# Fetching the experts' token rows with an indirect DMA instead of 0/1 products

## The chip, the cores and the metric

The kernel runs on one core of a Trainium2 chip. The metric is the device time of one execution in microseconds. The kernel before took 1614.17 us (median of 3 runs).

## The reference

A decoder trunk of two layers over 256 tokens of width 1024, in float32. The second layer's channel mixer is a top-2-of-8 expert SwiGLU:

```
logits = h @ w_router                                 # h = rms_norm(x)
top_val, top_idx = lax.top_k(logits, 2); top_w = softmax(top_val)
combine = sum(one_hot(top_idx, 8) * top_w[..., None], axis=-2)
for e in range(8):
    y += combine[..., e:e+1] * swiglu(h, w_gate_e[e], w_up_e[e], w_down_e[e])
x = x + y
```

The inner width of an expert is 3584. A final RMSNorm follows.

## The kernel before, in words

Every weight is float32 and is streamed once from device memory in units of 128 x 2048 elements (1 MiB), through a ring of slots (class `Stream`; its loads are issued on SyncE's queue, line 142). A unit is used in two halves. `do_split` cuts a half into a rounded part `wh` (ScalarE, line 152) and the rest `wl` (VectorE, line 153). `take` keeps four halves of splits ahead of the half that TensorE is about to use; five pairs of buffers hold them. `run` issues the products of a half: for each block of 512 columns one of the activations' high part and one of their low part with `wh` (lines 256 and 257), and after all blocks one with `wl` for each (line 261).

All instructions are issued in one order that the program itself plans. It counts an estimated clock: `run` calls `tick` after each block, with 512/1200 us for a pair of products with `wh` and 512/2400 for one with `wl`. Side work is put into a queue with `soon(wait, fn)` or `later(wait, fn)`, and the next `tick` at or past its time issues it between the weight products. Each engine then runs its own instructions in that order.

The experts come after both attention layers. `route` works out which tokens go to which expert, with a slot number for each. An expert has 7 chunks (j = 0 to 6) of 512 inner columns. In a chunk TensorE does two units for the gate, two for the up projection and two of the chunk before for the down projection (`down`). Four transposes turn the product g (`g_transpose`, line 884); lines 330 and 331 copy them out. Up to 128 tokens of an expert are worked on in one pass, as columns of `th` and `tl`, the high and the low part of the normed activations; the columns of even and of odd experts lie side by side.

What the next expert needs is prepared by `expert_prep` (lines 764 to 809), which is put into the side queue at the end of chunk j = 2. `select` makes the 0/1 matrix G (VectorE, line 772): token t is in slot s. `gather(q)`, called twice, multiplies the residual `xs` with G (line 780; two token blocks of 128 for each of 4 column blocks), which gives the rows of the expert's tokens, already turned; ScalarE and VectorE copy them into `th` and `tl` with the norm's gain (lines 784 and 787). `trans` turns G for the later scatter (line 802). `scales` multiplies G with `rc`, which holds each token's 1/rms and its weight for the expert (line 796), and VectorE copies the result (line 797). The planner's waits are

```
p1=4.0, p2=6.0, p3=8.0, p4=9.0      # gather(0), gather(1), trans, scales; select has 0.0
```

For the first expert the same steps run right behind `route`, ahead of all expert products.

GpSimd does small powers alone (line 327, 1/rms, and line 756, in the weights of the routing). Line 336 adds a mixer's output to `xs`; line 844 adds an expert's output to the result, which lies in a buffer of its own, so that `xs` stays as it is while the experts run.

Of the kernel before, what the change touches and what calls it, by code (L numbers as in the profile page):

```python
# [11 lines left out]
F32 = mybir.dt.float32  # L12
F32R = mybir.dt.float32r
BF16 = mybir.dt.bfloat16
I32 = mybir.dt.int32
# [4 lines left out]
P = 128  # L20
S = 256
D = 1024
# [87 lines left out]
C_LT = C_SIN + 128  # L110
C_IOTA = C_LT + 64
C_WR = C_IOTA + 128
C_ALL = C_WR + 64
B_TRI = 4 * 384
B_ONE = B_TRI + 128
B_ALL = B_ONE + 128
# [54 lines left out]
def trunk(ctx: ExitStack, tc: tile.TileContext, x, xt, wpre, wmoe, cst, cstb, gfin, out):  # L171
    nc = tc.nc
# [58 lines left out]
    def soon(wait, fn):  # L231
        put(urgent, wait, fn)
# [82 lines left out]
    def norm_half(gi, c):  # L315
# [6 lines left out]
        if gi != 3 or c == 0:  # L322
            soon(at + 1, lambda: sumsq(xs, c))

    def make_rstd():
        V.scalar_tensor_tensor(ms, ss[:, :, 0], EPS, ss[:, :, 1], op0=ALU.add, op1=ALU.add)  # L326
        nc.gpsimd.tensor_tensor(rstd, ms, nhalf, op=ALU.pow)  # L327
# [11 lines left out]
    def mixer(i, gnext, last=False):  # L339
        oo = [[], []]  # L340

        def out_unit(kh, c):
            unit((th, tl), oo[c], 4 * kh, 4, 512, kh == 0, kh == 1)

        with tc.tile_pool(name=f"mix{i}", bufs=2) as mp:
            with tc.tile_pool(name=f"att{i}", bufs=2, side="right", reuse_waits="tile") as ap:
                gates = attention(mp, ap)
            if last:
                moe_ring()
            projections(mp, gates)  # L350
            oo[0] += [mm_ps(), mm_ps()]
            out_unit(0, 0)
            oo[1] += [mm_ps(), mm_ps()]
            out_unit(0, 1)
            flush()
        if last:
            moe_open()
        for c in range(2):
            out_unit(1, c)
            flush()  # L360
            add_x(oo[c], c)
            norm_half(gnext, c)
            if c == 0 and last:
                soon(5.0, lambda: logits(0))

    def attention(mp, ap):
# [334 lines left out]
    def route():  # L701
        ep = M["ep"]

        def small(shape, name, dt=F32):
            return ep.tile(shape, dt, name=name, bufs=1)

        lp = M["lp"]
        lo, L, v8 = small([P, 2, 8], "lo"), small([P, 2, 8], "L"), small([P, 2, 8], "v8")
        R = ep.tile([P, 2, P], F32, name="G", tag="G")
        R1, R2 = (R[:, i, :].rearrange("p (b e j) -> p b e j", b=2, e=8) for i in range(2))  # L710
        rank = small([P, 2, 8], "rank")
        sel, slot = small([P, 2, 8], "sel", BF16), small([P, 2, 8], "slot")
        d1, z = small([P, 2, 8], "d1"), small([P, 2, 8], "z")
        rc = small([P, 2, 8, 2], "rc")
        warm(10)
        for b in range(2):
            A.activation(lo[:, b, :], lp[b][:, 8:16], AF.Copy, scale=rstd[:, b:b + 1])
        for b in range(2):
            V.scalar_tensor_tensor(L[:, b, :], lp[b][:, 0:8], rstd[:, b:b + 1], lo[:, b, :],
                                   op0=ALU.mult, op1=ALU.add)  # L720

        lt = C[:, C_LT:C_LT + 64].rearrange("p (e j) -> p e j", e=8).unsqueeze(1).to_broadcast([P, 2, 8, 8])
        lj = L.unsqueeze(2).to_broadcast([P, 2, 8, 8])
        le = L.unsqueeze(3).to_broadcast([P, 2, 8, 8])
        V.tensor_tensor(R2, lj, le, op=ALU.is_equal)
        V.tensor_tensor(R1, lj, le, op=ALU.is_gt)
        V.tensor_tensor(R2, R2, lt, op=ALU.mult)
        V.tensor_tensor(R1, R1, R2, op=ALU.add)
        V.tensor_reduce(rank, R1, axis=AX.X, op=ALU.add)
        V.tensor_scalar(sel, rank, 1.5, None, op0=ALU.is_lt)  # L730
        for b in range(2):
            V.tensor_copy(rc[:, b, :, 0], rstd[:, b:b + 1].to_broadcast([P, 8]))

        pp = mm_ps()
        tri, one = CB[:, 0:128], CB[:, 128:256]
        T.matmul(pp[:, 0:8], tri, sel[:, 0, :], start=True, stop=True)
        T.matmul(pp[:, 8:16], one, sel[:, 0, :], start=True, stop=False)
        T.matmul(pp[:, 8:16], tri, sel[:, 1, :], start=False, stop=True)
        T.matmul(pp[:, 16:24], one, sel[:, 0, :], start=True, stop=False)
        T.matmul(pp[:, 16:24], one, sel[:, 1, :], start=False, stop=True)  # L740
        V.tensor_tensor(slot, pp[:, 0:16].rearrange("p (b e) -> p b e", b=2), sel, op=ALU.mult)
        M["slot"], M["rc"] = slot, rc

        def weights():
            most, mosti = small([P, 1], "most"), small([P, 1], "mosti", I32)
            V.tensor_reduce(most, pp[:, 16:24], axis=AX.X, op=ALU.max)
            V.tensor_copy(mosti, most)
            M["most"] = mosti
            for b in range(2):
                V.max(v8[:, b, :], L[:, b, :])  # L750

            for b in range(2):
                V.tensor_scalar(d1[:, b, :], L[:, b, :], -2.0, v8[:, b, 0:1], op0=ALU.mult, op1=ALU.add)
            for b in range(2):
                V.tensor_scalar(z[:, b, :], d1[:, b, :], v8[:, b, 1:2], 88.0, op0=ALU.add, op1=ALU.min)
            nc.gpsimd.tensor_tensor(z, base_e.unsqueeze(2).to_broadcast([P, 2, 8]), z, op=ALU.pow)

        def weights2():
            V.tensor_scalar(z, z, 1.0, None, op0=ALU.add)
            V.reciprocal(z, z)  # L760
            V.tensor_tensor(rc[:, :, :, 1], z, sel, op=ALU.mult)
        return weights, weights2

    def expert_prep(e, off):

        ep, par = M["ep"], e % 2
        sl = {}

        def select():
            sl["G"] = ep.tile([P, 2, P], F32, name="G", tag="G")  # L770
            for b in range(2):
                V.tensor_scalar(sl["G"][:, b, :], C[:, C_IOTA:C_IOTA + P], float(off), M["slot"][:, b, e:e + 1],
                                op0=ALU.add, op1=ALU.is_equal)

        def gather(q):
            p = tp_ps()
            for i in range(4):
                k = 4 * q + i
                for b in range(2):
                    T.matmul(p[:, i * P:(i + 1) * P], xs[:, b, k * P:(k + 1) * P], sl["G"][:, b, :],  # L780
                             start=b == 0, stop=b == 1)
            for i in range(4):
                k = 4 * q + i
                A.activation(th[:, k, par * P:(par + 1) * P], p[:, i * P:(i + 1) * P], AF.Copy, scale=gain(3, k))
            for i in range(4):
                k = 4 * q + i
                V.scalar_tensor_tensor(tl[:, k, par * P:(par + 1) * P], p[:, i * P:(i + 1) * P], gain(3, k),
                                       th[:, k, par * P:(par + 1) * P].bitcast(F32),
                                       op0=ALU.mult, op1=ALU.subtract)

        def scales(c0, c1):
            if not c0:
                sl["sc"] = ep.tile([P, 2], F32, name="sc", tag="sc")
            p = tp_ps()
            for b in range(2):
                T.matmul(p[:, c0:c1], sl["G"][:, b, :], M["rc"][:, b, e, c0:c1], start=b == 0, stop=b == 1)
            V.tensor_copy(sl["sc"][:, c0:c1], p[:, c0:c1])

        def trans():
            p = tp_ps()  # L800
            for b in range(2):
                T.transpose(p[:, b * P:(b + 1) * P], sl["G"][:, b, :], ident)
            sl["GT"] = ep.tile([P, S], F32R, name="GT", tag="GT")
            A.activation(sl["GT"], p[:, 0:S], AF.Copy)

        M["slots", e] = sl
        both = (0, 1, 2) if e == 0 and not off else (0, 2)
        return [select, lambda: gather(0), lambda: gather(1), trans,
                *(lambda c=c: scales(*c) for c in zip(both, both[1:]))]

# [37 lines left out]
    def experts(off, first, weights=()):  # L848
# [11 lines left out]
        for e in range(NE):  # L860
            for j in range(NCH):
# [26 lines left out]
                    down(*prev, first and prev[0] == 0)  # L888
                prev = (e, j, gT)
                if j == 2 and e + 1 < NE:  # L890
                    for wait, fn in zip((0.0, PAR['p1'], PAR['p2'], PAR['p3'], PAR['p4']), expert_prep(e + 1, off)):
                        later(wait, fn)
                if j == NCH - 1:
                    drain()
# [2 lines left out]

    wrhl = base.tile([P, 8, 16], F32R, name="wrhl")
    M = {"ring": []}
    zeros = base.tile([P, P], BF16, name="zeros")  # L900
    V.memset(zeros, 0.0)

# [32 lines left out]
    flush()  # L935
    warm(4)
    make_rstd()
    logits(1)
    experts(0, True, route())

# [28 lines left out]
def constants(inputs):  # L969
# [14 lines left out]
    for i, n in enumerate(("norm_mix_0", "norm_ffn_0", "norm_mix_1", "norm_ffn_1")):  # L984
        c[:, C_G + 8 * i:C_G + 8 * i + 8] = inputs[n].reshape(8, P).T
    c[:, C_WR:C_WR + 64] = inputs["w_router_1"].reshape(8, P, NE).transpose(1, 0, 2).reshape(P, 64)
    b = np.zeros((P, B_ALL), np.float32)
    t = np.arange(S)[:, None]
    s = np.arange(S)[None, :]
    d = t - s  # L990
# [39 lines left out]
```

## Time and profile before

| | |
|---|---|
| runs | 1612.93, 1614.17, 1614.98 us |
| profiled execution | 1613.7 us |
| its span, first to last instruction | 1611.9 us |
| granted TensorE clock | 0.996 of full speed |
| busy TensorE / VectorE / ScalarE / GpSimd | 99% / 80% / 68% / 0% of the span |
| moved | 456.17 MB |

Times in rows are microseconds from the first instruction, and durations are in microseconds unless a column says ns. TensorE's products are pipelined, so a row's duration is longer than the distance to the next; that distance is what a product costs. PE is TensorE's products, PEld its loads of the stationary operand, DVE is VectorE, ACT is ScalarE, POOL is GpSimd and SP is SyncE, whose queue issues the transfers.

### The profile page before, as it was taken

Reading aid. Unit: us, or ns where it says so; the run is one execution under the profiler, and the core shown is the slowest. Engines: PE = TensorE matmul, PEld = TensorE weight load, DVE = VectorE, ACT = ScalarE, POOL = GpSimd, SP = SyncE. Lnnn points to the kernel's source line nnn. Section 1 sums busy time; section 2 is a strip of 40 time slices with the busy share of each in tenths; the row PEclk is TensorE's granted clock in tenths of the full one; section 3 lists DMA queues with packets and bytes.
Section 4 is the critical chain, followed back from the end, with each engine's and each line's share of the span. In section 5 each row is a group of like instructions: output and inputs, shape, how many; then the busy total and the mean of one; then the engine's idle time right before and its main releaser. Section 6 shows DMA issues by size and latency. Waiting matters only on the chain. (4 is left out here: it accounts for less than half of the span.)

```text
span 1611.9 us, 21105 instructions
## 1 busy us (share of the span) xinstructions
PE 1593.9 (99%) x7661; PEld 1306.4 (81%) x7661; DVE 1293.2 (80%) x1654; ACT 1096.8 (68%) x1413; POOL 6.6 (0%) x10
## 2 busy tenths in 40 slices
PE   9999999999999999999999999999999999999996
PEld 7777888888877878888888888888888888888885
DVE  6767655555786668899899889889889899889996
ACT  6556454445556448777787787787777777787784
POOL 0000000000000000000000000000000000000000
PEclk9999999999999999999999999999999999999998
DMA  8443546555434596899899899899999899989960
GB/s 333 171 144 141 182 174 198 185 185 200 167 144 148 217 395 246 332 365 361 336 378 355 339 368 353 335 361 360 340 375 352 341 368 363 362 335 364 361 261 28
DMA packets 64305, 456.17 MB, mean 283 GB/s; under 512 B 7104, under 2 KB 7360, under 8 KB 9408
## 3 DMA queue, kind: packets, MB, share of 16 engines
q1 hardware_dynamic: 64192, 454.73, 74.6%
q8 instruction: 62, 1.02, 0.2%
q14 instruction: 51, 0.42, 0.1%
HBM read 453.66 MB, written 1.05 MB: 282 GB/s over the span
## 5 line engine op out<-in xcount | busy, mean ns | idle before, releaser
L256 PE MATMUL mm<-wh,th 128*128 128x512 f32 (+1 forms) x1536 | 604.3, 395 | 2.0 <-ACT wh L152 2.0
L257 PE MATMUL mm<-wh,tl 128*128 128x512 f32 (+1 forms) x1536 | 592.3, 387 | 0.0
L153 DVE TENSOR_TENSOR wl<-raw,wh 128x1024 fp32r<-128x1024 f32 x376 | 447.2, 1221 | 135.3 <-ACT wh L152 134.8
L152 ACT ACTIVATE wh<-raw 128x1024 fp32r<-128x1024 f32 x376 | 390.9, 1058 | 148.3 <-PE mm L257 113.9
L261 PE MATMUL mm<-wl,th 128*128 128x512 f32 (+1 forms) x1536 | 451.5, 390 | 0.0
L153 DVE TENSOR_TENSOR wl<-ringa,wh 128x1024 fp32r<-128x1024 f32 x290 | 340.5, 1220 | 27.9 <-ACT wh L152 27.8
L256 PEld LDWEIGHTS mm<-wh,th 128*128 128x128 f32 x1536 | 289.2, 188 | 62.9 <-issue 5.7
L257 PEld LDWEIGHTS mm<-wh,tl 128*128 128x128 f32 x1536 | 289.6, 189 | 54.3
L261 PEld LDWEIGHTS mm<-wl,th 128*128 128x128 f32 x1536 | 281.5, 189 | 57.7 <-issue 2.0
L152 ACT ACTIVATE wh<-ringa 128x1024 fp32r<-128x1024 f32 x290 | 299.6, 1062 | 33.9 <-PE mm L257 16.1
L153 DVE TENSOR_TENSOR wl<-ringb,wh 128x1024 fp32r<-128x1024 f32 x188 | 217.7, 1220 | 19.4 <-ACT wh L152 19.4
L152 ACT ACTIVATE wh<-ringb 128x1024 fp32r<-128x1024 f32 x188 | 193.0, 1062 | 22.9 <-PE acc L257 13.5
L256 PE MATMUL acc<-wh,gT 128*128 128x512 f32 x224 | 87.4, 390 | 0.0
L257 PE MATMUL acc<-wh,gT 128*128 128x512 f32 x224 | 87.3, 390 | 0.0
L257 PE MATMUL acc<-wh,tmp 128*128 128x512 f32 x224 | 87.3, 390 | 0.0
L256 PE MATMUL acc<-wh,tmp 128*128 128x512 f32 x224 | 87.3, 390 | 0.0
L261 PE MATMUL acc<-wl,gT 128*128 128x512 f32 x224 | 69.2, 390 | 0.0
L261 PE MATMUL acc<-wl,tmp 128*128 128x512 f32 x224 | 69.2, 390 | 0.0
L867 ACT ACTIVATE g<-mm,sc 128x512 f32<-128x512 f32 x56 | 38.7, 691 | 39.4 <-PE mm L261 39.4
L261 PEld LDWEIGHTS acc<-wl,gT 128*128 128x128 f32 x224 | 42.1, 188 | 8.8
L257 PEld LDWEIGHTS acc<-wh,gT 128*128 128x128 f32 x224 | 42.1, 188 | 8.8
L257 PEld LDWEIGHTS acc<-wh,tmp 128*128 128x128 f32 x224 | 42.1, 188 | 8.7
(178 smaller groups left out, 1257.7 us busy)
## 6 DMA issues: line engine op xcount, KB each, us to landing
ringa<-in_wmoe_dram SPq DMA_DIRECT2D x144, 1024.0 KB, 6.1
raw<-in_wmoe_dram SPq DMA_DIRECT2D x96, 1024.0 KB, 5.8
ringb<-in_wmoe_dram SPq DMA_DIRECT2D x94, 1024.0 KB, 6.2
raw<-in_wpre_dram SPq DMA_DIRECT2D x91, 1024.0 KB, 4.8
late<-in_wmoe_dram SPq DMA_DIRECT2D x2, 1024.0 KB, 7.8
raw<-in_wpre_dram SPq DMA_DIRECT2D x2, 512.0 KB, 6.0
xs<-in_x_dram SPq DMA_DIRECT2D x2, 512.0 KB, 7.9
ringa<-in_wpre_dram SPq DMA_DIRECT2D x1, 1024.0 KB, 6.8
```

The source lines that it names most:

```text
L152: self.nc.scalar.activation(h, s, AF.Copy)
L153: self.nc.vector.tensor_tensor(l, s, h.bitcast(F32), op=ALU.subtract)
L256: T.matmul(o, xh(b), wh, start=start, stop=False)
L257: T.matmul(o, xl(b), wh, start=False, stop=False)
L261: T.matmul(o, xh(b), wl, start=False, stop=stop)
L867: A.activation(g, og, AF.Silu, scale=sl["sc"][:, 0:1])
```

## The change

The residual stream `xs` is also written to a buffer `xd` in device memory, in two halves, from GpSimd's queue. For experts 2 to 8, `scales` moves to the place right behind `select` and has a third column: the token's number. VectorE turns it into 32-bit integers, and GpSimd issues an indirect DMA that fetches the row of `xd` that each slot names into the tile `xg` (a slot without a token names row 0). `gather` then is four transposes of `xg` for each half in place of eight products with G. The waits of the preparation are new. The first expert is prepared as before.

```diff
+    def store_x(c):
+        nc.gpsimd.dma_start(M["xd"].rearrange("(b p) d -> p b d", p=P)[:, :, c * 512:(c + 1) * 512],
+                            xs[:, :, c * 512:(c + 1) * 512])
...
             add_x(oo[c], c)
             norm_half(gnext, c)
             if c == 0 and last:
+                M["xd"] = dram.tile([S, D], F32, name="xd")
+                store_x(0)
                 soon(5.0, lambda: logits(0))
...
-        rc = small([P, 2, 8, 2], "rc")
+        rc = small([P, 2, 8, 3], "rc")
...
             V.tensor_copy(rc[:, b, :, 0], rstd[:, b:b + 1].to_broadcast([P, 8]))
+            V.tensor_copy(rc[:, b, :, 2], C[:, C_TOK + b:C_TOK + b + 1].to_broadcast([P, 8]))
...
+        by_dma = e > 0
+
+        def fetch():
+
+            sl["xg"] = ep.tile([P, D], F32, name="xg", tag="xg", bufs=1)
+            nc.gpsimd.indirect_dma_start(out=sl["xg"], out_offset=None, in_=M["xd"],
+                                         in_offset=bass.IndirectOffsetOnAxis(ap=sl["idx"], axis=0))
+
         def gather(q):
             p = tp_ps()
             for i in range(4):
                 k = 4 * q + i
+                if by_dma:
+                    T.transpose(p[:, i * P:(i + 1) * P], sl["xg"][:, k * P:(k + 1) * P], ident)
+                    continue
                 for b in range(2):
...
-            V.tensor_copy(sl["sc"][:, c0:c1], p[:, c0:c1])
+            V.tensor_copy(sl["sc"][:, c0:min(c1, 2)], p[:, c0:min(c1, 2)])
+            if c1 > 2:
+                sl["idx"] = ep.tile([P, 1], I32, name="idx", tag="idx")
+                V.tensor_copy(sl["idx"], p[:, 2:3])
...
+        if by_dma:
+            return [select, lambda: scales(0, 3), fetch, lambda: gather(0), lambda: gather(1), trans]
...
-                    for wait, fn in zip((0.0, PAR['p1'], PAR['p2'], PAR['p3'], PAR['p4']), expert_prep(e + 1, off)):
+                    for wait, fn in zip((0.0, 2.0, 4.0, 20.0, 22.0, 24.0), expert_prep(e + 1, off)):
                         later(wait, fn)
...
     make_rstd()
+    store_x(1)
     logits(1)
     experts(0, True, route())
...
-    nc = bacc.Bacc("TRN2", target_bir_lowering=False, num_devices=1, dynamic_dma_scratch_size=1024)
+    nc = bacc.Bacc("TRN2", target_bir_lowering=False, num_devices=1, dynamic_dma_scratch_size=8192)
```

The rest of the diff adds two columns with the token numbers to the constants and opens the pool for `xd`.

## Rows read from the trace of the kernel before

**Rows 1.** Page, part 1: busy us (share of the span), instructions.

```profile
PE 1593.9 (99%) x7661; PEld 1306.4 (81%) x7661; DVE 1293.2 (80%) x1654; ACT 1096.8 (68%) x1413; POOL 6.6 (0%) x10
```

**Rows 2.** Waits of TensorE's products: us in total, times, longest.

```profile
PE mm L256 <- ACT wh L152: 2.0, 1, 2.0
PE tp L842 <- DVE tmp L835: 1.9, 8, 0.3
```

**Rows 3.** Timeline, TensorE: where chunks begin (start, us, instruction).

```profile
776.32 0.60 PE L884 MATMUL tp<-C,g 128*128 128x128 f32 x4
...
797.53 0.60 PE L884 MATMUL tp<-C,g 128*128 128x128 f32 x4
...
814.34 0.60 PE L884 MATMUL tp<-C,g 128*128 128x128 f32 x4
```

**Rows 4.** Busy time by stretch, one whole expert; last clock, DMA share, GB/s.

```profile
776.22:900.78 124.56, 124.33 (x580) 103.01 (x579) 112.62 (x116) 97.04 (x109) 0.00 (x0) 1.00 0.92 357
```

**Rows 5.** Groups by line and shape: busy us, mean ns | idle before.

```profile
L780 PE MATMUL tp<-G,xs 128*128 128x128 f32 x256 | 31.1, 275 | 0.7 <-DVE G L772 0.7
...
L772 DVE TENSOR_SCALAR G<-C,slot 128x128 f32<-128x128 f32 x16 | 3.8, 280 | 0.0
...
L797 DVE COPY sc<-tp 128x2 f32<-128x2 f32 x7 | 1.1, 152 | 0.0
```

**Rows 6.** Timeline, TensorE, fourth chunk: its first products and a gather.

```profile
776.67 0.48 PE L256 MATMUL mm<-wh,th 128*128 128x512 f32 x1
...
778.84 0.39 PE L257 MATMUL mm<-wh,tl 128*128 128x512 f32 x1
779.07 0.62 PE L261 MATMUL mm<-wl,th 128*128 128x512 f32 x2
...
781.34 1.95 PE L780 MATMUL tp<-G,xs 128*128 128x128 f32 x16
783.05 0.48 PE L256 MATMUL mm<-wh,th 128*128 128x512 f32 x1
```

**Rows 7.** Timeline, TensorE: four transposes of g and what follows.

```profile
831.15 0.60 PE L884 MATMUL tp<-C,g 128*128 128x128 f32 x4
831.51 0.48 PE L256 MATMUL mm<-wh,th 128*128 128x512 f32 x1
```

**Rows 8.** Timeline, VectorE, fourth chunk, around `select`.

```profile
778.53 1.22 DVE L153 TENSOR_TENSOR wl<-ringa,wh 128x1024 fp32r<-128x1024 f32 x1 [0.26 <-ACT wh L152]
779.68 0.47 DVE L772 TENSOR_SCALAR G<-C,slot 128x128 f32<-128x128 f32 x2
780.07 3.49 DVE L153 TENSOR_TENSOR wl<-ringa,wh 128x1024 fp32r<-128x1024 f32 x3
```

**Rows 9.** Timeline, the first expert's `select` and gather.

```profile
601.94 0.48 DVE L772 TENSOR_SCALAR G<-C,slot 128x128 f32<-128x128 f32 x2
602.37 3.81 PE L780 MATMUL tp<-G,xs 128*128 128x128 f32 x32 [0.68 <-DVE G L772]
```

**Rows 10.** Timeline, GpSimd and VectorE, 586 to 625.

```profile
586.20 1.29 DVE L336 TENSOR_TENSOR xs<-xs,mm 128x512 f32<-128x512 f32 x2 [1.08 <-PE mm L261]
...
598.24 0.70 POOL L327 TENSOR_TENSOR rstd<-ms,nhalf 128x2 f32<-128x2 f32 x1 [192.11 <-DVE ms L326]
...
619.63 2.89 POOL L756 TENSOR_TENSOR z<-base_e,z 128x16 f32<-128x16 f32 x1 [20.69 <-DVE z L755]
...
620.06 4.62 DVE L153 TENSOR_TENSOR wl<-raw,wh 128x1024 fp32r<-128x1024 f32 x4
```

**Rows 11.** DMA: a queue (packets, MB, share), one issue (KB, us to landing).

```profile
q1 hardware_dynamic: 64192, 454.73, 74.6%
...
xs<-in_x_dram SPq DMA_DIRECT2D x2, 512.0 KB, 7.9
```

**Rows 12.** Busy time by stretch, while the ring was filled; last GB/s.

```profile
560.00:565.00 5.00, 5.00 (x26) 4.17 (x25) 4.93 (x8) 1.28 (x2) 0.00 (x0) 1.00 1.03 433
```

More of the change, by code (lines that the diff above doesn't have):

```diff
@@ L112 @@
 C_WR = C_IOTA + 128
-C_ALL = C_WR + 64
+C_TOK = C_WR + 64
+C_ALL = C_TOK + 2
 B_TRI = 4 * 384
@@ L899, in trunk @@
     M = {"ring": []}
+    dram = ctx.enter_context(tc.tile_pool(name="dram", bufs=1, space=bass.MemoryType.DRAM))
     zeros = base.tile([P, P], BF16, name="zeros")
@@ L986, in constants @@
     c[:, C_WR:C_WR + 64] = inputs["w_router_1"].reshape(8, P, NE).transpose(1, 0, 2).reshape(P, 64)
+    c[:, C_TOK:C_TOK + 2] = np.arange(S, dtype=np.float32).reshape(2, P).T
     b = np.zeros((P, B_ALL), np.float32)
```

## The prediction

> **What bounds the kernel now.** First the busy times. TensorE is busy for nearly the whole span, VectorE for four fifths of it [rows 1], and what TensorE waits for adds up to a few microseconds, at single places [rows 2]. So a microsecond that leaves TensorE's queue is a microsecond of the run, as long as the other engines keep up, and a microsecond for which TensorE waits is lost.
>
> Next the stage that the change touches: the eight experts. The transposes of g (line 884) mark the beginning of each chunk on TensorE. A chunk with nothing beside its weights takes 814.34 - 797.53 = 16.81 us; the fourth chunk of an expert (j = 3), in which the next expert is prepared, takes 797.53 - 776.32 = 21.21 us [rows 3]. Its 4.40 us more are what the preparation costs. A whole expert takes 124.56 us, and in it TensorE is busy for 124.33 and VectorE for 112.62 [rows 4]. VectorE has a tenth of the time in hand, no more.
>
> **What is removed.** One `gather` is 16 instructions on TensorE (8 products, 2 passes each; 256 instructions in all [rows 5]). The one shown begins at 781.34, and the next weight product begins at 783.05: 1.71 us [rows 6]. There are 2 in each of 7 experts, 14 in all; the first expert keeps its products.
>
> **What replaces it.** Four transposes of 128x128 float32 against the identity. The same four stand in the kernel already, those of g: from 831.15 to the next weight product at 831.51, 0.36 us [rows 7]. Each gather so becomes 1.35 us shorter, and 14 of them are 18.9 us. ScalarE's and VectorE's eight copies out of PSUM in each gather stay as they are.
>
> **What is moved, and the wait it makes.** The preparation gets other times. Before, the order was select at 0, the gathers at 4 and 6, `trans` at 8, `scales` at 9 of the planner's microseconds; now it is select 0, `scales` 2, fetch 4, gathers 20 and 22, `trans` 24. The planner counts 0.427 us for each pair of products with `wh` and 0.213 for one with `wl`, 1.28 for half a unit. A wait of 4.0 was reached in the fourth half, after its first pair (3.84 + 0.43), and there it stands in the trace: six products of each half from 776.67, then 781.34 [rows 6]. A wait of 2.0 is reached at 1.28 + 0.85 = 2.13, in the second half after both `wh` pairs: behind the product that began at 778.84, so at 779.07.
>
> `scales` multiplies by the selection matrix G, which VectorE writes in `select`. In what state is G then? VectorE is in order, and ahead of select stands the split that the first half has asked for; that one waits for ScalarE's `wh` and ends at 779.75. Select's first half begins at 779.68 [rows 8] and takes 0.28 [rows 5], to 779.96. For the first expert, where TensorE waited for the same G, its product began at 602.37, when the first half of G had ended at 601.94 + 0.28: 0.15 us later [rows 9]. So `scales` can start at about 780.1 and not at 779.07. TensorE, which is in order, stands for **1.0 us, and some 0.1 more because here G is the operand that is loaded first: 1.1 us**. Behind that wait are all weight products. Nothing gives it back: no wait is there that it could shorten [rows 2]. All seven prepared experts run these same instructions in this order; so I count seven times 1.1 = 7.7 us. Bounds: nothing, if VectorE gets to select a microsecond sooner; 1.4 us (9.8 in all) if TensorE waits for both halves of G and their load. I take 1.1, since the chain ahead of select starts from TensorE's own transposes at 776.32 and isn't touched.
>
> **Edits that I cost at nothing, and their cover.** The third column of `scales`: the product has 3 columns for 2. The copy of the index, 0.15 us by the copies there are [rows 5], is on VectorE, which is far enough ahead: the split that ends at 779.75 is read by TensorE four halves after 776.67, not before 782, and without a gather in this chunk its lead grows by the stall. The `trans` and the two late gathers come one chunk later at nearly the same places in a chunk, where VectorE kept up before with the same copies; TensorE now comes 1.35 us sooner to the end of each, which eats about that much of a lead of some 3 us. If that lead were gone, each missing microsecond would cost 7. The fetch is issued by GpSimd, which has nothing queued but two small powers in this stage (line 327, and line 756 for the first expert) [rows 10]. The copy of the residual, twice 512 KB, goes through the same queue: the first half has its data at 586.20 + 1.29 = 587.49, ten microseconds before the power of line 327 at 598.24 [rows 10], and the second is issued behind that power. Only its second half falls on the chain that everything waits for, from 598 to 606. I count 0.3 us for both stores and the two copies in `route`, bounded by 0 and by 2.9, the longest GpSimd instruction of the trace [rows 10].
>
> **The fetch itself** must land before the first late gather. The index is there at about 781.6: VectorE first does the split that begins at 780.07 and lasts 1.2 [rows 8], then two copies. The gather comes at 20.05 planner units. That is 16.81 + 1.1 + an estimated 0.5 for `scales` until the next chunk, then 5.1 to the second `wh` pair of its fourth half (4.67 as before plus 0.45): about 800.2. So there are 18.6 us. The trace has no transfer issued by GpSimd. The nearest row is the load of x, the same 512 KB, 7.9 us from issue to landing [rows 11]: 10.7 us to spare. The far bound is that the 128 rows pass one engine one after another. A packet took on average 0.746 x 16 x 1611.9 / 64192 = 0.30 us [rows 11], 128 of them 38.4 us, 19.8 too late. I take 7.9: the loads of that size in this kernel are spread over the engines, and so will this one be.
>
> **The sum.** -18.9 + 7.7 + 0.3 = -10.9 us against the profiled execution's 1613.7: **1603 us**, 0.7% faster. That execution is 0.5 us below the median of the runs, which changes nothing here. An expert then takes 124.56 - 2.70 + 1.1 = 122.96 us. What a measurement can tell from no change is about 0.2%, 3.2 us.
>
> **Rivals.**
> *No stall, the full gain.* If select is done in time, the time is 1613.7 - 18.9 + 0.3 = 1595. For it: only that VectorE has a tenth of its time free. Against: the chain in [rows 8]. Chance 0.12.
>
> *The fetch is late (slower).* Its place is the first late gather, where TensorE would wait for the rows. It decides from a fetch of 18.6 + 1.6 = 20.2 us, where the gain of 1.6 an expert is used up. For it: beside it the weights' queue has the engines busy for 92% of the time [rows 4]; half of the 128 places, those without a token, all name row 0. Against: 7.9 us for the same bytes. On one engine it would give 1603 + 7 x 19.8 = 1742. Chance 0.10.
>
> *GpSimd and VectorE get in each other's way.* If writing the descriptors stopped VectorE for longer than its lead (3.4 us from 779.75 to the `wl` products four halves on, and 1.1 from the stall), TensorE would stand for the rest; at 7.9 us, as long as a whole load, that is 3.4 an expert, and 1603 + 24 = 1627. Against: during the 2.89 us of GpSimd's power VectorE's splits went on, four in 4.62 us [rows 10]. Chance 0.08, most of it in smaller sizes of 1605 to 1612.
> The Trainium skill has the rule for this in "SBUF — State Buffer", section "Who interferes with whom": VectorE instructions with two operands in SBUF contend with GpSimd instructions that read SBUF, and the one that came second waits. By that rule GpSimd, which reads the 128 indices, and the splits, which read two tiles, would have to take turns; the four splits beside the power do not show VectorE slowed.
>
> *The memory is the bound, and nothing is gained.* An expert moves 42 units of 1 MiB, 44.04 MB; with the fetch it is 44.56 MB in 122.96 us, 362 GB/s, beside 357 shown now [rows 4]. If 357 were the ceiling, an expert would stay at 124.8 and the time at about 1614. Against: 433 GB/s in a stretch in which the slots of the ring were filled [rows 12]. Chance 0.05.
> The skill's "DMA: Bandwidth & Descriptors", section "Specifications", gives about 358 GB/s for the memory of one core; by that figure the estimate would be 124.5 us an expert and no gain. The 433 of the trace stand above it, and I go by the trace.
>
> **How the numbers follow.** The forecast has 0.60; with the stall between 0.6 and 1.4 us and the stores between 0 and 2.9 it lies between 1599 and 1607. No stall 0.12, late fetch 0.10, GpSimd against VectorE 0.08, memory 0.05, and 0.05 for what I don't see. The range goes down to 1594 to hold the full gain, and up to 1609 for a small share of the contention; beyond it are the late fetch, the ceiling and the unseen, 2 in 10. Faster by over 0.2%: 0.60 + 0.12 and most of the contention and a part of the unseen, 0.81. Within: the ceiling and a little, 0.07. Slower: 0.12.
>
> **What would show it.** Right: in the fourth chunk of an expert a wait of TensorE for G of line 772 (by its name, before the products with `rc`), about 1.1 us, seven times; that chunk some 18.4 us long; the transposes of `xg` at 0.36 us for four, with no wait for a DMA ahead of them; the chunk after it some 18 us instead of 16.81. Wrong: waits of TensorE for `xg`, splits of VectorE that are longer than 1.22 us beside the fetch, waits of TensorE for `wh` or `wl`, or ScalarE waiting for weights.

## The result, and the profile after

The changed kernel took 1602.23 us (median of 4 runs, 1601.25 to 1603.41), the kernel before 1614.58 (4 runs, 1612.93 to 1615.12) beside it. The ratio is 0.9926, 95% interval 0.9908 to 0.9943: 12.35 us less, 0.7%. The forecast was 1603 us, -10.9.

The profiled execution took 1603.41 us, with a span of 1601.0. From the page of the changed kernel, part 1, to be held against [rows 1]:

```profile
PE 1575.7 (98%) x7493; PEld 1284.7 (80%) x7493; DVE 1292.3 (81%) x1663; ACT 1093.0 (68%) x1413; POOL 17.0 (1%) x19
```

TensorE has 168 products fewer: 224 passes of products have gone and 56 transposes have come. What it now waits for, longest first; the columns are those of [rows 2]. Lines have moved: 780 writes G, 815 is the product of `scales`, 796 the transposes of `xg`, 788 the fetch, 154 VectorE's part of a split, 908 the transposes of g, 257, 258 and 262 the weight products.

```profile
PE tp L815 <- DVE G L780: 6.2, 7, 0.9
PE mm L257 <- ACT wh L153: 3.0, 2, 1.7
PE tp L866 <- DVE tmp L859: 1.9, 8, 0.3
```

The first line is new: seven waits for G. There is none for `xg`. In the timeline of TensorE the fourth and the fifth chunk of an expert look like this (the same columns as [rows 3] and [rows 6]):

```profile
775.66 0.60 PE L908 MATMUL tp<-C,g 128*128 128x128 f32 x4
...
778.17 0.39 PE L258 MATMUL mm<-wh,tl 128*128 128x512 f32 x1
779.44 0.58 PE L815 MATMUL tp<-rc,G 128*128 128x3 f32 x4 [0.88 <-DVE G L780]
779.88 0.48 PE L262 MATMUL mm<-wl,th 128*128 128x512 f32 x1
...
794.03 0.60 PE L908 MATMUL tp<-C,g 128*128 128x128 f32 x4
...
799.49 0.60 PE L796 MATMUL tp<-C,xg 128*128 128x128 f32 x4
799.84 0.71 PE L262 MATMUL mm<-wl,th 128*128 128x512 f32 x2
...
812.05 0.60 PE L908 MATMUL tp<-C,g 128*128 128x128 f32 x4
```

A product begins 0.23 us after the one before it, so `scales` could have begun at 778.40; it began at 779.44, 1.04 us later. Four transposes take 799.84 - 799.49 = 0.35 us. The fourth chunk is 794.03 - 775.66 = 18.37 us long, the fifth 812.05 - 794.03 = 18.02, together 36.39; before they were 21.21 + 16.81 = 38.02 [rows 3].

VectorE's own rows around `select`, to be held against [rows 8], and GpSimd's fetch:

```profile
777.87 1.22 DVE L154 TENSOR_TENSOR wl<-ringa,wh 128x1024 fp32r<-128x1024 f32 x1 [0.25 <-ACT wh L153]
779.01 0.47 DVE L780 TENSOR_SCALAR G<-C,slot 128x128 f32<-128x128 f32 x2
779.41 1.22 DVE L154 TENSOR_TENSOR wl<-ringa,wh 128x1024 fp32r<-128x1024 f32 x1
780.54 0.15 DVE L816 COPY sc<-tp 128x2 f32<-128x2 f32 x1
780.61 0.15 DVE L819 CAST idx<-tp 128x1 int32<-128x1 f32 x1
780.68 1.23 DVE L154 TENSOR_TENSOR wl<-ringa,wh 128x1024 fp32r<-128x1024 f32 x1
...
781.51 1.24 POOL L788 DMA_INDIRECT xg<-xd,idx  x1 [121.49 <-PE mm L258]
```

Select begins 779.01 - 775.66 = 3.35 us after the transposes of g; before it was 779.68 - 776.32 = 3.36 [rows 3, 8]. The index is there at 780.76, GpSimd's descriptors at 782.75. From the part on DMA (columns as in [rows 11]) and from the view of line 788:

```profile
xg<-xd,idx POOLq DMA_INDIRECT x7, 7.8
```

```profile
DMA to landing us min/median/max: 5.4/7.8/10.3
```

Counted from 781.51, the rows were there at 791.8 at the latest, and the first transposes of `xg` come at 799.49.

### The profile page after: what moved, and what is told of

The parts are those of the page before. It is cut to its first block, busy times and chain, and to the rows that moved or that the text cites. A ratio compares the mean times of both kernels' runs of the same rounds, so it can differ in the third digit from the quotient of the medians.

```text
span 1601.0 us, 20811 instructions
## 1 busy us (share of the span) xinstructions
PE 1575.7 (98%) x7493; PEld 1284.7 (80%) x7493; DVE 1292.3 (81%) x1663; ACT 1093.0 (68%) x1413; POOL 17.0 (1%) x19
## 5 line engine op out<-in xcount | busy, mean ns | idle before, releaser
L262 PEld LDWEIGHTS acc<-wl,tmp 128*128 128x128 f32 x224 | 42.0, 188 | 8.8
```

Of the source, the lines that this page charges most:

```text
L262: T.matmul(o, xh(b), wl, start=False, stop=stop)
```

## The experiments

The kernel before that was run beside these kernels took 1615.13 us (8 runs) for the first four, 1615.34 (7 runs) for the next three. The changed kernel was timed beside 1614.58, so a difference between its 1602.23 us and one of these medians is good to somewhat under a microsecond. Each edit is against the changed kernel unless it says otherwise.

**The scales later.** In the planner's waits:

```diff
-                    for wait, fn in zip((0.0, 2.0, 4.0, 20.0, 22.0, 24.0), expert_prep(e + 1, off)):
+                    for wait, fn in zip((0.0, 4.0, 6.0, 20.0, 22.0, 24.0), expert_prep(e + 1, off)):
```

> The changed kernel, with the scales at 4.0 and the fetch at 6.0 planner microseconds in place of 2.0 and 4.0; all else as changed. My theory: the wait of TensorE for G, 1.04 us from start to start in each of seven chunks of the changed kernel, is lost time and goes away, since 4.0 is the place where the old gather met no wait; the fetch, issued some 2 us later, still lands well ahead of the gather. 7 x 1.04 = 7.3 us less than 1602.2: 1595 us, and no row of TensorE waiting for G there. Rival: the wait only gave VectorE time that it needs, and comes back as waits for wh or wl: 1601 to 1603.

Measured: 1593.95 us (4 runs, 1593.69 to 1593.98); to the kernel before 0.9867, interval 0.9851 to 0.9884. No row of TensorE waiting for G in `scales` is left. The timeline of TensorE in this kernel:

```profile
773.05 0.60 PE L908 MATMUL tp<-C,g 128*128 128x128 f32 x4
...
777.83 0.39 PE L258 MATMUL mm<-wh,tl 128*128 128x512 f32 x1
778.06 0.50 PE L815 MATMUL tp<-rc,G 128*128 128x3 f32 x4
778.42 0.48 PE L257 MATMUL mm<-wh,th 128*128 128x512 f32 x1
```

`scales` follows the product ahead of it by 0.23 us and takes 0.36. The fourth chunk is 17.25 us long, 1.15 less than the changed kernel's usual 18.40; seven times that is 8.0 of the 8.3 us between the medians. The wait was lost time, and VectorE did not need it. This is the fastest version of the study.

**The products late.** The steps in the changed order, with the old products:

```diff
-                if by_dma:
-                    T.transpose(p[:, i * P:(i + 1) * P], sl["xg"][:, k * P:(k + 1) * P], ident)
-                    continue
...
-            return [select, lambda: scales(0, 3), fetch, lambda: gather(0), lambda: gather(1), trans]
+            return [select, lambda: scales(0, 3), lambda: None, lambda: gather(0), lambda: gather(1), trans]
...
-                store_x(0)
...
-    store_x(1)
```

> The changed kernel's order of steps (select 0, scales 2 with three columns, gathers 20 and 22, trans 24), but with the 0/1 products in place of the transposes, no copy of the residual and no fetch. My theory: 14 gathers of 1.71 us in place of 0.36, so 18.9 us more than the changed kernel, 1621 us, which is 7 us slower than the kernel before, the price of the wait for G. Rival: it is the later place of the gathers that pays, and the products cost little there: 1602 to 1610.

Measured: 1622.07 us (5 runs, 1620.61 to 1623.18); ratio 1.0042, interval 1.0027 to 1.0056. The fifth chunk is 20.66 us long instead of 18.03, the fourth stays at 18.40. So the new order by itself makes the kernel slower, through the same wait for G, and the whole gain comes with the transposes. Its TensorE rows of the two chunks:

```profile
779.23 0.60 PE L904 MATMUL tp<-C,g 128*128 128x128 f32 x4
783.01 0.58 PE L811 MATMUL tp<-rc,G 128*128 128x3 f32 x4 [0.88 <-DVE G L779]
797.62 0.60 PE L904 MATMUL tp<-C,g 128*128 128x128 f32 x4
803.08 1.95 PE L795 MATMUL tp<-G,xs 128*128 128x128 f32 x16
807.15 1.95 PE L795 MATMUL tp<-G,xs 128*128 128x128 f32 x16
818.28 0.60 PE L904 MATMUL tp<-C,g 128*128 128x128 f32 x4
```

**Transposes alone.** Against the kernel before:

```diff
                 k = 4 * q + i
+                if e > 0:
+                    T.transpose(p[:, i * P:(i + 1) * P], xs[:, e % 2, k * P:(k + 1) * P], ident)
+                    continue
                 for b in range(2):
```

> The kernel before with its own order of steps, in which experts 2 to 8 turn 128 rows of the residual as they lie in SBUF, with no selection: the choice of the tokens is left out, and there is no copy and no fetch. My theory: TensorE's part alone, 14 x 1.35 = 18.9 us less than the kernel before, 1595 to 1596 us. Together with the run that puts the scales later it tells whether stores and fetch cost anything: if both come to the same time, they don't. Rival: VectorE has no room for gathers that are over sooner, and TensorE waits for wh or wl in the fourth chunk: 1600 or more.

Measured: 1595.36 us (4 runs, 1594.47 to 1597.35); ratio 0.9879, interval 0.9862 to 0.9895: 19.8 us less than the kernel before, where 18.9 were expected. The fourth chunk is 18.54 us long, 2.67 less than before, and seven times that is 18.7; the other chunks are unchanged. The run with the later scales, which has both stores and all fetches, is not slower than this one, which has none (its other chunks are each 0.02 us shorter, about 1 us in all; see the plain chunk below): where the rows come from costs nothing that these runs can tell.

**The gathers early.**

```diff
-                    for wait, fn in zip((0.0, 2.0, 4.0, 20.0, 22.0, 24.0), expert_prep(e + 1, off)):
+                    for wait, fn in zip((0.0, 2.0, 4.0, 8.0, 10.0, 12.0), expert_prep(e + 1, off)):
```

> The changed kernel with the gathers at 8 and 10 and trans at 12 in place of 20, 22 and 24. The index is there at 4.8 us after the chunk begins, GpSimd issues at 5.5, and the rows land 7.8 us later in the middle (5.4 to 10.3), at about 13.3; TensorE comes to the first transposes at about 10.2. My theory: it waits some 3 us in each of seven chunks for xg, with all weight products behind it: 1602 + 7 x 3 = 1624 us, between 1607 and 1641 by the spread of the landings. Rival: TensorE's queue and the lead of the splits hide it and the time stays within 3 us of 1602.

Measured: 1640.99 us (4 runs, 1633.56 to 1649.84); ratio 1.0152, interval 1.0103 to 1.0200. The waits are where the theory put them, and a little longer than its 3 us:

```profile
PE tp L796 <- DMA xg<-xd,idx: 26.6, 7, 4.8
PE tp L815 <- DVE G L780: 6.2, 7, 0.9
```

But they explain 27 us, and the median is 38.8 above the changed kernel's; the profiled execution took 1645.88 us, 43.7 above that median. The rest is TensorE's clock. The fourth chunk of the first expert is 26.95 us long. Its busy times by stretch (busy us of PE, PEld, DVE, ACT, POOL, each with its count; then granted clock, DMA share, GB/s): up to the wait, the wait, up to the end of the second gather, the rest. The last line is the whole of the one chunk with a short wait.

```profile
653.26:663.96 10.70, 9.82 (x47) 7.76 (x45) 8.07 (x12) 7.47 (x9) 1.26 (x1) 1.00 0.94 325
663.96:668.77 4.81, 0.16 (x2) 0.03 (x1) 2.19 (x2) 0.56 (x1) 0.00 (x0) 0.86 0.95 362
668.77:674.20 5.43, 5.43 (x18) 4.46 (x18) 2.26 (x5) 2.08 (x5) 0.00 (x0) 0.50 0.30 127
674.20:680.21 6.01, 6.01 (x30) 4.91 (x29) 4.56 (x8) 5.20 (x9) 0.00 (x0) 1.00 0.51 176
1170.44:1192.35 21.91, 18.92 (x91) 15.16 (x90) 17.16 (x26) 15.34 (x23) 1.23 (x1) 1.00 0.83 316
```

The clock falls in the stretch of the wait (0.86 over all of it) and stands at 0.50, 1.2 GHz, for the 5.43 us behind it, in which products come at 0.43 us instead of 0.23. Without any wait for `xg` such a chunk would take an estimated 16.79 + 1.61 + 1.24 = 19.64 us (a plain chunk, and what the fourth and the fifth of the changed kernel have more). The stretch of 4.81 us, in which TensorE stood for 4.65 by its row, so cost 26.95 - 19.64 = 7.31. In the chunk with the short wait, 2.11 us by TensorE's row, the clock stayed at 1.00, and the chunk cost 21.91 - 19.64 = 2.27. The first transposes behind the shortest of the six long waits, and behind that short one:

```profile
1056.90 1.09 PE L796 MATMUL tp<-C,xg 128*128 128x128 f32 x4 [3.55 <-DMA xg<-xd,idx]
...
1183.39 0.63 PE L796 MATMUL tp<-C,xg 128*128 128x128 f32 x4 [2.11 <-DMA xg<-xd,idx]
```

In all six chunks with a wait of 3.55 us or more these four took 1.08 or 1.09 us, instead of 0.60 in the changed kernel: the clock had fallen in each. Over the seven chunks the lengths add up to 179.5 us, 42.0 more than 7 x 19.64.

**The gathers in the middle.** The waits of the list are 0, 2, 4, 12, 14, 16.

```diff
-                    for wait, fn in zip((0.0, 2.0, 4.0, 20.0, 22.0, 24.0), expert_prep(e + 1, off)):
+                    for wait, fn in zip((0.0, 2.0, 4.0, 12.0, 14.0, 16.0), expert_prep(e + 1, off)):
```

> The changed kernel with the gathers at 12 and 14 and trans at 16, between the changed kernel's 20, 22, 24 and the 8, 10, 12 of the early run. TensorE comes to the first transposes 14.8 us after the chunk's first product; the fetch is issued at 5.6 and lands 5.4 to 10.3 us later, at 11.0 to 15.9. My theory: most of the seven find their rows there, one or two wait up to 1 us, and a wait that short lets the granted clock stay: 1602 to 1604 us. Rival: the landing is late often enough, or the clock falls even at a wait of a microsecond, and it takes 1605 to 1615.

Measured: 1606.86 us (4 runs, 1605.09 to 1609.83), which is the rival's range and not mine; ratio 0.9949, interval 0.9933 to 0.9966. In the profiled execution (1606.13 us) the row of TensorE's waits for `xg` is small, and the fourth chunks are between 19.35 and 19.94 us:

```profile
PE tp L796 <- DMA xg<-xd,idx: 0.6, 2, 0.4
```

The fetch landed there after 5.6 to 9.8 us. So the landing was late in two of seven, by little. The seven fourth and fifth chunks are together 1.1 us longer than the changed kernel's; another 1.0 us of this execution stands behind the last chunk, where nothing of the edit runs. A place at the edge of the landing's spread so loses a part of the gain, but how much of the 4.6 us between the medians comes from late landings isn't shown: the longer executions have no trace.

**Two fetches.**

```diff
-            nc.gpsimd.indirect_dma_start(out=sl["xg"], out_offset=None, in_=M["xd"],
-                                         in_offset=bass.IndirectOffsetOnAxis(ap=sl["idx"], axis=0))
+            for n in ("xg2", "xg"):
+                t = sl["xg"] if n == "xg" else ep.tile([P, D], F32, name="xg2", tag="xg2", bufs=1)
+                nc.gpsimd.indirect_dma_start(out=t, out_offset=None, in_=M["xd"],
+                                             in_offset=bass.IndirectOffsetOnAxis(ap=sl["idx"], axis=0))
```

> The changed kernel with each fetch issued twice, first into a second tile that nothing reads, then into xg (the descriptors' scratch is 6144 in place of 8192 so that the tile fits). My theory: GpSimd and the transfers are hidden; GpSimd works 1.24 us more in each of seven chunks, the rows land a few us later (the 8 us of one fetch, and no more than as much again, before 800), VectorE's splits stay at 1.22 us, and the time is within 3 us of 1602.2. Rival: GpSimd's descriptors or the 0.5 MB more for each expert take VectorE's or the weights' time: each microsecond that TensorE lacks counts seven times, so 1605 to 1612.

Measured: 1601.71 us (4 runs, 1601.17 to 1602.50); ratio 0.9914, interval 0.9898 to 0.9931. Groups by line and shape of this kernel:

```profile
L154 DVE TENSOR_TENSOR wl<-ringa,wh 128x1024 fp32r<-128x1024 f32 x290 | 341.2, 1221 | 36.4 <-ACT wh L153 36.3
...
L790 POOL DMA_INDIRECT xg<-xd,idx x14 | 22.9, 1636 | 752.2 <-DVE idx L821 715.0 <-PE mm L258 35.1 <-issue 2.1
```

GpSimd took 1.64 us for each issue, and the rows landed 10.5 us after it in the middle (at most 13.4), later than one fetch alone; the splits stay at 1.22 us, and the time stays.

**No stores.**

```diff
-                store_x(0)
...
-            nc.gpsimd.indirect_dma_start(out=sl["xg"], out_offset=None, in_=M["xd"],
+            nc.gpsimd.indirect_dma_start(out=sl["xg"], out_offset=None, in_=x,
...
-    store_x(1)
```

> The changed kernel with the copy of the residual left out: the fetch reads the rows of the kernel's input x, which is other data of the same shape and place. My theory: the stores cost nothing that counts, 1601 to 1603 us; where TensorE's granted clock is low between 598 and 602 us it is by the time at which the routing falls and not by the stores, for the run with the late products showed it without any store (0.71) and the run with the later scales had the stores and 1.00. Rival: the stores hold GpSimd or VectorE up in the routing and cost the 1.5 us by which the first gather came later after 1/rms in the changed kernel: the clock is full there in this run, and the time about 1600.5.

Measured: 1603.78 us (4 runs, 1602.44 to 1607.29); ratio 0.9933, interval 0.9917 to 0.9950. That is a little above the forecast range, and not below the changed kernel. From the first transposes of g to the last this kernel took 952.87 us, the changed kernel 952.83; taking the stores away gives nothing back. The clock was full here between 598 and 602 us, as the rival had it, but the stores don't decide it (below).

**The plain chunk.** A chunk with nothing beside its weights takes 16.81 us in the kernel before and 16.79 in all kernels with the new order, the products late among them. Two parts of the change were put into the kernel before, alone:

```diff
-    nc = bacc.Bacc("TRN2", target_bir_lowering=False, num_devices=1, dynamic_dma_scratch_size=1024)
+    nc = bacc.Bacc("TRN2", target_bir_lowering=False, num_devices=1, dynamic_dma_scratch_size=8192)
```

> The kernel before with the descriptors' scratch of the changed kernel (8192 in place of 1024), nothing else. Chunks of an expert with nothing beside their weights take 16.81 us in the kernel before and 16.79 in the changed one, also where products stand in place of the fetch. If the scratch does it, such chunks take 16.79 us here; if not, 16.81. The time is within 2 us of 1614 either way.

```diff
-C_ALL = C_WR + 64
+C_ALL = C_WR + 66
```

> The kernel before with the two more columns of constants of the changed kernel, which nothing reads, and which move the tiles behind them by 8 bytes. If the place of the tiles makes the 0.02 us of a plain chunk, such chunks take 16.79 us here; if not, 16.81. The time is within 2 us of 1614 either way.

Both keep 16.81 us (1613.51 and 1614.99 us, one run each). Neither is the cause; which other part is stays open.

## Why the prediction was right, point by point

*What bounds.* TensorE's queue set the time in every run, its waits included. What left it (e3's 19.8 us) and what stood in it (e1's 8.3 us) came out in the medians almost one for one, and work on GpSimd, on the DMA engines and in VectorE's lead did not.

*The transposes.* 0.36 us for four, forecast; 0.35 measured. The term of 18.9 us is shown by the transposes alone (19.8 between the medians, 7 x 2.67 = 18.7 in the chunks) and from the other side by the late products (1622.07 - 1602.23 = 19.8, and 7 x 2.63 = 18.4 in the chunks). Where the medians' other microsecond comes from isn't shown.

*The wait for G.* Forecast 1.1 us in each of seven experts. From start to start it is 1.04, and the four products with `rc` take 0.44 us behind the wait instead of 0.36 without it; what the fourth chunk gives back without the wait is 1.15. The forecast's 0.1 for the load of G stood on no row, and 1.04 + 0.08 is what the rows put in its place. By the medians it is 8.3 us in all, 7.7 forecast. The rival "no stall" fell, since select stands where it stood, 3.35 us behind the transposes of g.

*The two chunks.* Forecast some 18.4 and 18, measured 18.37 and 18.02. An expert takes about 122.8 us instead of the forecast 122.96.

*The fetch.* Forecast 7.9 us by the load of x, measured 7.8 (5.4 to 10.3), against 799.49 - 781.51 = 18.0 us of room. The rival "late fetch" didn't happen here. Its price was mis-sized: I put a microsecond at a microsecond. The early gathers show that a stretch of 4.81 us with a wait cost 7.31, since the clock fell with it.

*GpSimd and VectorE.* The rival had VectorE stopped. VectorE's splits beside the descriptors took 1.22 and 1.23 us, as before, and with twice the fetches 1.22; what became longer was GpSimd's work. In the changed kernel the descriptors began at 781.51, inside a split that ended at 780.68 + 1.23 = 781.91, and took 1.24 us. With the later scales they began just ahead of a split and took 0.97 us; in the expert before it 1.07, and 0.94 in each later one:

```profile
781.17 0.97 POOL L788 DMA_INDIRECT xg<-xd,idx  x1 [120.51 <-PE mm L262]
...
781.29 2.36 DVE L154 TENSOR_TENSOR wl<-ringa,wh 128x1024 fp32r<-128x1024 f32 x2 [0.86 <-ACT wh L153]
```

With two fetches the first began 0.89 us before the end of a split, and took 1.70:

```profile
779.05 1.23 DVE L154 TENSOR_TENSOR wl<-ringa,wh 128x1024 fp32r<-128x1024 f32 x1
...
779.39 1.70 POOL L790 DMA_INDIRECT xg<-xd,idx  x1 [119.13 <-DVE idx L821]
```

Less what was left of the split, 1.24 becomes 0.84 and 1.70 becomes 0.81. So the rows read as GpSimd waiting for the split that was under way; no run tests that alone, or shows which of GpSimd's accesses waited. It cost nothing, since the rows had time to spare. The rule of the Trainium skill ("SBUF — State Buffer", "Who interferes with whom"), by which one of the two would wait, and that the one that came second, agrees with these rows; it doesn't show as a longer split in these traces.

*Memory.* The stretch of one expert moved 365 GB/s, above the 357 of before [rows 4]. Busy time by stretch of the changed kernel:

```profile
775.66:898.43 122.77, 121.66 (x555) 100.08 (x554) 112.48 (x117) 96.54 (x109) 1.24 (x1) 1.00 0.97 365
```

The Trainium skill's figure of about 358 GB/s ("DMA: Bandwidth & Descriptors", "Specifications"), by which nothing would have been gained, is not the limit here. The loads of the weights landed 7.0 us after their issue instead of some 6, and nothing waited for them in the experts.

*The sum.* In the two profiled executions the spans differ by 1611.9 - 1601.0 = 10.9 us, which is the forecast number, but partly by chance. From the first transposes of g (623.12 before, 624.21 after) to the last (1588.16 and 1577.04) it is 12.2 us less: 7 x 1.6 in the two chunks, and about 1 us from plain chunks that are 0.02 us shorter, a term that the forecast didn't have. Ahead of that the changed kernel's profiled execution lost 1.1 us in the routing, where ten products took 4.02 us at a lower granted clock (last section) and 2.33 in the kernel before; behind the last chunk it lost 0.2. Nothing shows of the 0.3 us forecast for the stores: with the later scales, stores included, the first transposes of g came at 622.78, and without stores at 623.62.

## What to carry to other kernels

Where an engine's queue is the bound, work that can come from a DMA engine is worth what it took in that queue, if its place is put outside the spread of the landing (here 10 us, and 13 with two fetches in a row) and not at its middle. When a step is moved ahead, look at who writes its operand and at what stands ahead of that writer: here 2 planner microseconds made a wait in seven places, and moving the consumer back by as much took 8.3 us off and made the best version, 1593.95 us, 1.3% below the kernel before. And test a transfer's cost by doubling it and by leaving it out; neither moved the time here beyond the noise, which is what hidden means.

## What the runs showed of the hardware that I had not expected

In dense work, a stretch of 4.81 us in which TensorE waited was followed by 5.43 us at a granted clock of 0.50 (1.2 GHz), a wait of 2.11 us by none. That late operand so cost half as much again as its lateness (7.31 us), the other hardly more than its own (2.27). The Trainium skill ("TensorE: Matmul & The Clock Gate", "What's actually happening") says that the half clock is the state of rest and that activity releases it; these rows agree.

The same fall stands in the routing, between 598 and 602 us, in some executions and not in others. Ten products with zeros (line 932) that keep TensorE busy there took 4.02 us in the changed kernel's trace and 2.33 in that of the later scales; the first expert's gather began at 603.46 and at 602.04:

```profile
598.65 4.02 PE L932 MATMUL mm<-zeros 128*128 128x512 bf16 x10
...
603.46 2.80 PE L799 MATMUL tp<-G,xs 128*128 128x128 f32 x23 [0.68 <-DVE G L780]
```

```profile
598.75 2.33 PE L932 MATMUL mm<-zeros 128*128 128x512 bf16 x10
...
602.04 3.81 PE L799 MATMUL tp<-G,xs 128*128 128x128 f32 x32 [0.68 <-DVE G L780]
```

The granted clock of the stretch 598 to 602 was 0.60 with the change, 0.64 and 0.69 with early and middle gathers, 0.71 with the late products, which have no store, and 0.76 with two more columns of constants in the kernel before; it was 1.00 with the later scales and with two fetches, which have the stores. It was 1.00 too in the kernel before, with the transposes alone and without stores. So neither the stores nor the fetch decide it. Nor does the time at which these products come, as the run without stores had it: there they began at 599.57 and took 2.33 us, and with the late products at 599.62 and took 4.02. What decides it is open.
